# One decoder step on one core: x's spill and four early loads tied to the order of the program, the dt product and the first scores later

## The chip, the cores and the metric

The kernel runs on one core of one Trainium2 chip. The metric is the device time of one execution in microseconds (us). Each kernel is run several times and the median counts.

## The reference

One step of a hybrid decoder layer, in float32, for 256 prompt rows and 8 × 4 = 32 sample rows at once (T = 288 rows, model width 2048). `h` is the normed input. `w_in` projects it to z, x|B|C, dt, q, k, v. Two parallel halves follow: a state-space half (causal convolution, then a scan with a state per head) and a sliding-window attention half. Their joined output goes through `w_out`; then come a cross attention over a memory and a SwiGLU feed-forward, each with its residual.

```python
proj = h @ lp['w_in']
z, xbc, dt_raw, q, k, v = jnp.split(proj, [s1, s2, s3, s4, s5], axis=-1)
xbc, conv_new = causal_conv(xbc, conv0, lp['conv_w'], lp['conv_b'])
dt = jax.nn.softplus(dt_raw + lp['dt_bias'])
y, ssm_new = ssd_scan(xs, dt, a, bm, cm, ssm0)          # state per head
y = rmsnorm((y + xs * d_skip) * silu(z), gate_norm)
att = swa_banded(q, k, v, sinks)                        # prompt rows
att = swa_cached(q, kcat, vcat, pos, k_pos, sinks)      # sample rows, with the key cache
out = concat([y, att]) @ lp['w_out']
x = x + out
x = x + cross_attn(rmsnorm(x), mk, mv, lp)
x = x + ffn(rmsnorm(x), lp)
```

## The kernel before, in words

**Layout and matmuls.** Activations lie with the 2048 model columns on partitions: 16 tiles of 128 × 288. Every weight product is made of three passes (`mm3`, lines 164 to 168): the weight and the activation are each split into a high and a low part in a shorter float format, and lo·hi, hi·hi and hi·lo are summed. A weight **chunk** is 128 × 1024 numbers (512 KB). `wload` (line 139) loads it into a `raw` buffer (3 of them), ACT casts it to `hi` (line 156), DVE subtracts to get `lo` (the helper on line 79); there are 4 buffers of each. A chunk feeds 24 matmuls.

**Order.** The program is written as a sequence, and a scheduler reorders it: it has a time model, gives each engine and queue a fixed order by priority (place in the program, less an offset), and puts in an instruction as soon as the model says that its inputs are there. On the chip each engine then works through its own list in that order and waits where an input is late. Weight loads have an offset of 4000 (they go as soon as a `raw` buffer is free), the splits one of 70. Loads without such an offset, but with nothing to wait for, go as early as a buffer of their pool is free.

**Postponed work.** `later(n, fn)` (line 122) queues `fn` for n steps ahead, and each weight chunk that has been used is one step (`gemm_w`, line 179, which runs half of what is due at a chunk's end and the rest after the next chunk's first half). So the small work of attention and states stands between the matmuls of later chunks.

**The stages around the change.**
- Lines 336 to 360: x is loaded in four column parts, transposed by PE (`split_x`, line 277), split into hi and lo (`xh`, `xl`), and kept in float32 in 16 buffers `xb` (`xst`). Line 291 writes each of these to DRAM (`xspill`) by a DMA that POOL issues; line 1005 reads them back for the residual, long after. In the same loop the chunks of k, v and of the first queries are used.
- Lines 410 to 487: dt. `wdt` (16 columns) is loaded by SP (line 415) and scaled on DVE, 16 small matmuls with `xst` follow (line 421), then `dt_natural`, `dt_softplus` and `dt_sums` are postponed. `dt_sums` writes `csrow` to DRAM; `decay` (line 752) reads it back.
- Lines 494 to 563: queries in four pairs (`rp`). The first pair's product is made with k and v; the other three take 4 chunks each. `swa_prompt` turns each query tile (lines 496 to 500, DVE and POOL) and postpones `scores` (line 503: 8 matmuls on line 511, softmax on DVE and ACT), then `values` and `combine`, which writes `att`. `att` takes over the 16 `xb` buffers of `xst`.
- Line 566: `swa_sample`, the sample rows' attention. It loads the key cache (line 571), transposes it, and stores it to the output by POOL (line 575).
- Line 662: `conv_state` loads the convolution state (line 666) and transposes it.
- Lines 847 to 916: `sample_state(g)` goes through the state of the 8 sample sequences in four tiles of 4 × 256 KB (g, hb): `load` (line 850, loads on line 854), `grow` (POOL: state × decay, written to `m` from `ld` by the helper on line 79), `trans` (PE transposes, DVE adds, SP stores on line 893), `read`.
- `ssd` (line 780) makes, per head pair, `decayed` inputs on POOL (`s` from `s`, 128 × 256), which the PE products on lines 814 and 820 wait for.

The buffers `ld` (6) serve x, `wdt`, the convolution state, the key cache, the states and later the memory. All loads named here are issued by SP, which also issues all weight loads and most stores.

Of the kernel before, what the change touches and what calls it, by code (L numbers as in the profile page):

```python
# [8 lines left out]
F32 = mybir.dt.float32  # L9
# [6 lines left out]
P = 128  # L16
# [30 lines left out]
def tile_hymba_step(ctx: ExitStack, tc: tile.TileContext, I: dict, O: list, stop: int = 99):  # L47
# [24 lines left out]
    def psum(tag="ps"):  # L72
        return tl(p_ps, [P, 512], F32, "ps")
# [41 lines left out]
    def transpose(out, in_):  # L115
        k = in_.shape[0]
        b = in_.base_partition() if callable(in_.base_partition) else in_.base_partition
        nc.tensor.transpose(out, in_, ident[b:b + k, 0:k])  # L118

    pend, clock = [], [0]  # L120
# [156 lines left out]
    def split_x(cp, pcs):  # L277
        pss = []
        for k in range(4):
            kk = cp * 4 + k  # L280
            ps = psum()
            pss.append(ps)
            for t3 in range(3):
                n = P if t3 < 2 else TS
                transpose(ps[:, t3 * P:t3 * P + n], pcs[t3][:n, k * P:(k + 1) * P])
            act(xh[kk], ps[:, :T], AF.Copy, scale=nwcol(V_MIX, kk))
            stt(xl[kk], ps[:, :T], nwcol(V_MIX, kk), f32(xh[kk]), ALU.mult, ALU.subtract)
        for k in range(4):
            st = tl(p_xb, [P, T], F32, "xb")
            nc.vector.tensor_copy(st, pss[k][:, :T])  # L290
            nc.gpsimd.dma_start(xspill[cp * 4 + k], st)
            xst.append(st)
# [35 lines left out]

    # keys, values and the first queries
    wq = w_in.rearrange("(k p) c -> p k c", p=P)  # L330
# [78 lines left out]

    # dt path  # L410
    nat = ts(192).rearrange("p (c j h) -> p c j h", c=3, j=4)
    csrow = tc.dram_tile([16, T], F32, name="csrow")
    wdt = tl(p_ld, [P, 512], F32, "ld").rearrange("p (k h) -> p k h", h=32)
    nc.gpsimd.memset(wdt, 0.0)
    nc.sync.dma_start(wdt[:, :, 0:16], wq[:, :, O_DT:O_DT + 16])
    tt(nc.vector, wdt, wdt, vT[:, 0:KC].unsqueeze(2).to_broadcast([P, KC, 32]), ALU.mult)
    nc.gpsimd.memset(nat, 0.0)
    pdt = psum()
    for k in range(KC):
        j = k % 4  # L420
        nc.tensor.matmul(pdt[32 * j:32 * j + 32, :T], wdt[:, k], xst[k], start=(k < 4), stop=(k >= KC - 4))
    dtT = ts()
    nc.scalar.copy(dtT, pdt[:, :T])
    dx, dy, dz, dp = ts(192).rearrange("p (i c h) -> i p c h", i=4, c=3)
# [60 lines left out]

    later(1, dt_natural)
    later(7, dt_sums)

    # prompt sliding-window attention
    att = [(tl(p_xb, [P, T], F32R, "xb"), tl(p_xb, [P, T], F32R, "xb")) for _ in range(8)]  # L490
# [3 lines left out]
    def swa_prompt(r, pq):  # L494
# [59 lines left out]

        later(1, scores)

# [7 lines left out]

    # sample sliding-window attention
    def swa_sample():
        ms = cst[:, C_MS:C_MS + 144]
        kcT, vc = [], []
        for hb in range(2):
            k_ = tl(p_ld, [P, 4, P], F32, "ld")  # L570
            nc.sync.dma_start(k_, ck[4 * hb:4 * hb + 4].rearrange("b t g d -> t b (g d)"))
            ps = psum()
            for b in range(4):
                transpose(ps[:, b * P:(b + 1) * P], k_[:, b])
            nc.gpsimd.dma_start(o_sk[0, 4 * hb:4 * hb + 4, 0:124].rearrange("b t g d -> t b (g d)"), k_[4:128])
            kt_ = tm()
            nc.scalar.copy(kt_, ps)
            v_ = tm()
            nc.sync.dma_start(v_.rearrange("p (b c) -> p b c", b=4),
                                cv[4 * hb:4 * hb + 4].rearrange("b t g d -> t b (g d)"))  # L580
            nc.gpsimd.dma_start(o_sv[0, 4 * hb:4 * hb + 4, 0:124].rearrange("b t g d -> t b (g d)"),
                                v_[4:128].rearrange("p (b c) -> p b c", b=4))
            kcT += [kt_[:, b * P:(b + 1) * P] for b in range(4)]
            vc += [v_[:, b * P:(b + 1) * P] for b in range(4)]
# [64 lines left out]
        later(3, stage2)  # L649

    later(7, swa_sample)
    if stop <= 1:
# [4 lines left out]

    # state-space heads
    xc = [ts() for _ in range(12)]
    scT = ts().rearrange("p (c k) -> p c k", k=24)  # L660

    def conv_state():
        ps = psum()
        for cp in range(3):
            scv = tl(p_ld, [P, 512], F32, "ld")
            nc.sync.dma_start(scv[:24], I["state_conv"][0, :, :, 512 * cp:512 * cp + 512].rearrange("b k c -> (b k) c"))
            for c in range(4):
                transpose(ps[:, (4 * cp + c) * 24:(4 * cp + c) * 24 + 24], scv[:24, c * P:(c + 1) * P])
        nc.scalar.copy(scT.rearrange("p a b -> p (a b)"), ps[:, :288])
# [172 lines left out]

    # sample states
    bm = cst[:TS, C_BM:C_BM + 8]
    ssm = I["state_ssm"][0].rearrange("b (i f) p n -> i (f p) b n", f=2)
    osm = o_sssm[0].rearrange("b (i f) p n -> i (f p) b n", f=2)
    def sample_state(g):
        py = psum()

        def load(hb):  # L850
            h0s = []
            for i4 in range(4):
                h0 = tl(p_ld, [P, 4, P], F32, "ld")
                nc.sync.dma_start(h0, ssm[4 * g + i4, :, 4 * hb:4 * hb + 4])
                h0s.append(h0)
# [72 lines left out]

    # gate and group norm
    ymx = []  # L930
# [149 lines left out]

    # cross attention
    oT = [(tl(p_xb, [P, T], F32R, "xb"), tl(p_xb, [P, T], F32R, "xb")) for h in range(4)]
# [186 lines left out]

    # feed-forward  # L1270
    NF = DFF // P
# [45 lines left out]

    # final norm
    ydst = [o_yp[0, 0:P], o_yp[0, P:TP], o_ys.rearrange("b t d -> (b t) d")]
# [110 lines left out]
```

## Time and profile before

| | |
|---|---|
| median of 3 runs | 1395.02 us (1394.44 to 1398.37) |
| profiled execution, span from first to last instruction | 1393.4 us; no other time of its own is given |
| PE / DVE / ACT / POOL busy | 99% / 58% / 46% / 13% of the span |
| DMA | 241.17 MB, mean 173 GB/s |

How to read it: PE's busy share counts a matmul as busy from its start to a modelled end, so 99% is not a rate. The rate is read from the start times of the matmuls, and what stands still from the idle times in brackets. The granted clock is a share of TensorE's 2.4 GHz; 0.50 is 1.2 GHz.

### The profile page before, as it was taken

What the parts mean: (1) busy time and instruction counts of PE and PEld (TensorE: products, weight loads), DVE (VectorE), ACT (ScalarE), POOL (GpSimd) and SP (SyncE); (2) the same over time, 40 slices, a digit from 0 to 9 for tenths busy, and PEclk for the clock granted to TensorE, in tenths of its full rate; (3) what the DMA queues carried; (4) which work ended last, traced back from release to release, by engine and by line L of the source; (5) the groups of instructions that cost most, each with busy time, mean ns of one, the idle gap of its engine ahead of it and who ended that gap; (6) DMA issues with size and microseconds to landing.
All of it is one profiled execution on the core that took longest, in us unless ns stands there. A gap on an engine that the chain in (4) does not pass through costs nothing.

```text
span 1393.4 us, 26184 instructions
## 1 busy us (share of the span) xinstructions
PE 1373.9 (99%) x10637; PEld 1338.3 (96%) x10637; DVE 809.1 (58%) x1341; ACT 635.1 (46%) x998; POOL 177.2 (13%) x273
## 2 busy tenths in 40 slices
PE   9899999999999999999999999999999999999997
PEld 8799988899998899999999999999999999999997
DVE  6777798766666559544544544444454554545554
ACT  6355776554555556433433433333343333434332
POOL 4311476403220113000000000000000000000110
PEclk9999999999999999999999999999999999999999
DMA  9655547667657745555555545555555555555552
GB/s 291 169 157 144 150 120 231 187 195 206 185 192 243 228 155 161 166 166 167 162 170 166 166 160 164 165 165 174 167 167 167 167 167 167 167 159 167 166 167 91
DMA packets 249856, 241.17 MB, mean 173 GB/s; under 512 B 12778, under 2 KB 240528, under 8 KB 249736
## 3 DMA queue, kind: packets, MB, share of 16 engines
q1 hardware_dynamic: 246120, 232.43, 54.9%
q0 software_dynamic: 3584, 7.06, 1.7%
q8 instruction: 83, 1.36, 0.4%
q14 instruction: 37, 0.30, 0.1%
q10 hardware_dynamic: 32, 0.01, 0.0%
HBM read 227.59 MB, written 11.85 MB: 172 GB/s over the span
## 4 chain that ended last, share of the span: by engine, by line
PE 87%; DVE 5%; DMA 2%; ACT 2%; issue 2%; POOL 0%; SPq 0%; DVEq 0%; ACTq 0%; POOLq 0%
PE mm L166 27%; PE mm L167 27%; PE mm L168 27%; PE ps L118 2%; DMA raw<-in_w_in_dram 2%; DVE lo L79 2%; DVE s L82 1%; ACT hi L156 1%; PE ps L511 1%; DVE xa L82 1%; DVE m L769 0%; PE ps L1134 0%; DVE s L79 0%; ACT L85 0%; ACT s L85 0%
## 5 line engine op out<-in xcount | busy, mean ns | idle before, releaser
L79 DVE TENSOR_TENSOR lo<-raw,hi 128x1024 fp32r<-128x1024 f32 (+1 forms) x413 | 483.0, 1172 | 472.7 <-ACT hi L156 466.3
L156 ACT CAST hi<-raw 128x1024 fp32r<-128x1024 f32 (+1 forms) x413 | 410.9, 998 | 547.4 <-PE mm L168 435.6
L166 PE MATMUL mm<-xa,lo 128*128 128x288 f32 x2016 | 601.2, 298 | 0.0
L167 PE MATMUL mm<-xa,hi 128*128 128x288 f32 x2016 | 597.5, 296 | 0.0
L168 PE MATMUL mm<-xa,hi 128*128 128x288 f32 x2016 | 591.0, 293 | 0.0
L166 PEld LDWEIGHTS mm<-xa,lo 128*128 128x128 f32 x2016 | 378.4, 188 | 4.7 <-issue 3.8
L168 PEld LDWEIGHTS mm<-xa,hi 128*128 128x128 f32 x2016 | 379.7, 188 | 0.7 <-issue 0.6
L167 PEld LDWEIGHTS mm<-xa,hi 128*128 128x128 f32 x2016 | 379.4, 188 | 1.0 <-issue 0.7
L79 POOL TENSOR_TENSOR ssum<-ssum,ls 128x288 f32<-128x288 f32 x43 | 46.9, 1091 | 880.0 <-ACT ls L85 879.1
L166 PE MATMUL mm<-ls,lo 128*128 128x288 f32 x512 | 152.0, 297 | 0.0
L168 PE MATMUL mm<-ls,hi 128*128 128x288 f32 x512 | 151.4, 296 | 0.0
L167 PE MATMUL mm<-ls,hi 128*128 128x288 f32 x512 | 151.1, 295 | 0.0
L167 PE MATMUL mm<-xb,hi 128*128 128x288 f32 x448 | 132.5, 296 | 0.0
L166 PE MATMUL mm<-xb,lo 128*128 128x288 f32 x448 | 132.1, 295 | 0.0
L168 PE MATMUL mm<-xb,hi 128*128 128x288 f32 x448 | 132.1, 295 | 0.0
L166 PEld LDWEIGHTS mm<-ls,lo 128*128 128x128 f32 x512 | 96.2, 188 | 0.1
L168 PEld LDWEIGHTS mm<-ls,hi 128*128 128x128 f32 x512 | 96.2, 188 | 0.0
L167 PEld LDWEIGHTS mm<-ls,hi 128*128 128x128 f32 x512 | 96.1, 188 | 0.1
L168 PEld LDWEIGHTS mm<-xb,hi 128*128 128x128 f32 x448 | 84.6, 189 | 0.2 <-DVE xb L79 0.2
L166 PEld LDWEIGHTS mm<-xb,lo 128*128 128x128 f32 x448 | 84.5, 189 | 0.1
L167 PEld LDWEIGHTS mm<-xb,hi 128*128 128x128 f32 x448 | 84.0, 188 | 0.1
L79 DVE TENSOR_TENSOR xT<-xT,mm 128x288 f32<-128x288 f32 x64 | 28.2, 448 | 39.1 <-PE mm L168 36.2
(304 smaller groups left out, 1211.3 us busy)
## 6 DMA issues: line engine op xcount, KB each, us to landing
raw<-in_w_gate_dram SPq DMA_DIRECT2D x88, 512.0 KB, 3.6
raw<-in_w_up_dram SPq DMA_DIRECT2D x88, 512.0 KB, 3.6
raw<-in_w_down_dram SPq DMA_DIRECT2D x80, 512.0 KB, 3.5
raw<-in_w_in_dram SPq DMA_DIRECT2D x43, 512.0 KB, 3.9
raw<-in_w_in_dram SPq DMA_DIRECT2D x34, 256.0 KB, 5.3
raw<-in_w_out_dram SPq DMA_DIRECT2D x32, 256.0 KB, 4.1
raw<-in_w_out_dram SPq DMA_DIRECT2D x16, 512.0 KB, 3.6
ld<-in_state_ssm_dram SPq DMA_DIRECT2D x16, 256.0 KB, 4.1
```

Source lines behind the costliest of these rows:

```text
L79: eng.tensor_tensor(out=out, in0=in0, in1=in1, op=op)
L82: nc.vector.scalar_tensor_tensor(out=out, in0=in0, scalar=s, in1=in1, op0=op0, op1=op1)
L118: nc.tensor.transpose(out, in_, ident[b:b + k, 0:k])
L156: nc.scalar.copy(h_, src)
L166: nc.tensor.matmul(ps, wl, xh, start=start, stop=False)
L167: nc.tensor.matmul(ps, wh, xh, start=False, stop=False)
L168: nc.tensor.matmul(ps, wh, xl, start=False, stop=stop)
L511: nc.tensor.matmul(pss[g][:, oc], qa[gs, qc], kT[gs, kc], start=True, stop=True)
```

## The change

A helper `in_turn` calls the scheduler's `keep_in_program_order`: the instruction may stand on its engine's list only behind the instruction of that engine that the program named just before it. It adds an order, not a wait. With it:
- x's spill leaves `split_x` and POOL. It is postponed from the dt product, two tiles per step over 8 steps, issued by SP, each in turn.
- The dt product (16 matmuls and a copy) is postponed by 2 chunks, and `dt_natural` and `dt_sums` count from there.
- The first scores of each query tile come 2 chunks after it, not 1.
- The loads of `wdt`, of the key cache, of the convolution state and of the first state tile (g = 0, hb = 0) are in turn. The key cache's load gets a function of its own, 4 steps ahead of `swa_sample`.

```diff
+    def in_turn(ins):
+        tc.keep_in_program_order(ins)
...
             nc.vector.tensor_copy(st, pss[k][:, :T])
-            nc.gpsimd.dma_start(xspill[cp * 4 + k], st)
...
-    nc.sync.dma_start(wdt[:, :, 0:16], wq[:, :, O_DT:O_DT + 16])
+    in_turn(nc.sync.dma_start(wdt[:, :, 0:16], wq[:, :, O_DT:O_DT + 16]))
...
-    pdt = psum()
-    for k in range(KC):
-        j = k % 4
-        nc.tensor.matmul(pdt[32 * j:32 * j + 32, :T], wdt[:, k], xst[k], start=(k < 4), stop=(k >= KC - 4))
     dtT = ts()
-    nc.scalar.copy(dtT, pdt[:, :T])
+    def dt_product():
+        pdt = psum()
+        for k in range(KC):
+            j = k % 4
+            nc.tensor.matmul(pdt[32 * j:32 * j + 32, :T], wdt[:, k], xst[k], start=(k < 4), stop=(k >= KC - 4))
+        nc.scalar.copy(dtT, pdt[:, :T])
+        for k in range(KC):
+            later(1 + k // 2, lambda k=k: in_turn(nc.sync.dma_start(xspill[k], xst[k])))
+        later(1, dt_natural)
+        later(7, dt_sums)
...
-    later(1, dt_natural)
-    later(7, dt_sums)
+    later(2, dt_product)
...
-        later(1, scores)
+        later(2, scores)
...
+    def cache_keys():
+        for hb in range(2):
+            k_ = tl(p_ld, [P, 4, P], F32, "ld")
+            in_turn(nc.sync.dma_start(k_, ck[4 * hb:4 * hb + 4].rearrange("b t g d -> t b (g d)")))
+            kcs.append(k_)
...
+    later(3, cache_keys)
     later(7, swa_sample)
...
-            nc.sync.dma_start(scv[:24], I["state_conv"][0, :, :, 512 * cp:512 * cp + 512].rearrange("b k c -> (b k) c"))
+            in_turn(nc.sync.dma_start(scv[:24], I["state_conv"][0, :, :, 512 * cp:512 * cp + 512].rearrange(
+                "b k c -> (b k) c")))
...
-                nc.sync.dma_start(h0, ssm[4 * g + i4, :, 4 * hb:4 * hb + 4])
+                ld = nc.sync.dma_start(h0, ssm[4 * g + i4, :, 4 * hb:4 * hb + 4])
+                if g == 0 and hb == 0:
+                    in_turn(ld)
```

## Rows read from the trace of the kernel before

**Rows 1.** Busy time by stretch: us; PE, PEld, DVE, ACT, POOL; clock; DMA share; GB/s.
```profile
0.00:60.00 60.00, 55.47 (x394) 50.08 (x394) 40.61 (x105) 31.62 (x70) 20.04 (x38) 1.00 0.95 263
60.00:65.00 5.00, 4.33 (x22) 3.10 (x23) 4.59 (x22) 2.37 (x12) 3.76 (x8) 0.68 0.16 47
60.00:100.00 40.00, 39.33 (x309) 35.17 (x310) 32.45 (x124) 20.63 (x68) 9.58 (x17) 0.96 0.48 142
180.00:200.00 20.00, 16.86 (x120) 14.97 (x119) 19.95 (x34) 12.59 (x25) 17.02 (x18) 0.87 0.44 130
195.00:200.00 5.00, 3.85 (x12) 2.84 (x13) 4.95 (x4) 0.92 (x4) 5.00 (x5) 0.50 0.48 128
200.00:205.00 5.00, 5.00 (x36) 4.52 (x35) 4.94 (x18) 3.98 (x8) 1.84 (x3) 0.82 0.26 87
```

**Rows 2.** Timeline of PE: start, us, line, operation, count; in brackets idle before, releaser.
```profile
49.61 0.30 PE L167 MATMUL mm<-xa,hi 128*128 128x288 f32 x1
49.75 0.29 PE L168 MATMUL mm<-xa,hi 128*128 128x288 f32 x1
...
60.67 0.93 PE L511 MATMUL ps<-s,s 64*128 64x128 f32 x8 [4.06 <-DVE s L79]
...
107.80 0.92 PE L118 MATMUL ps<-cst,ld 24*128 24x24 f32 x12
...
195.06 1.22 PE L814 MATMUL ps<-s,s 128*128 128x256 f32 x2 [2.04 <-POOL s L79]
...
219.93 0.60 PE L118 MATMUL ps<-cst,ld 128*128 128x128 f32 x4
```

**Rows 3.** Chain of waits, 40 to 60 us: start, us, what.
```profile
50.62 7.98 DMA raw<-in_w_in_dram
...
59.34 0.69 DVE lo L79
```

**Rows 4.** The page's DMA issues: operation, count, KB each, us to landing.
```profile
xspill<-xb POOLq DMA_DIRECT2D x16, 144.0 KB, 5.1
out_dram<-ld POOLq DMA_DIRECT2D x2, 248.0 KB, 10.2
```

**Rows 5.** Timeline of SP's queue: start, us, line, operation, count.
```profile
30.88 0.45 SPq L415 DMA_DIRECT2D ld<-in_w_in_dram  x1
...
46.70 0.37 SPq L854 DMA_DIRECT2D ld<-in_state_ssm_dram  x1
...
89.85 0.82 SPq L754 DMA_DIRECT2D csb<-csrow  x2
92.66 14.18 SPq L147 DMA_DIRECT2D raw<-in_w_in_dram  x4
108.25 1.47 SPq L854 DMA_DIRECT2D ld<-in_state_ssm_dram  x3
...
209.11 0.47 SPq L705 DMA_DIRECT2D out_dram<-s  x1
```

**Rows 6.** Timeline of POOL: start, us, line, operation, count; idle before, releaser.
```profile
146.08 1.57 POOL L581 DMA_DIRECT2D out_dram<-m  x1 [14.82 <-DMA m<-in_cache_swa_v_dram]
...
188.55 5.65 POOL L79 TENSOR_TENSOR m<-ld,s 128x512 f32<-128x512 f32 x4
194.16 4.96 POOL L79 TENSOR_TENSOR s<-s,s 128x256 f32<-128x256 f32 x4
...
223.76 0.45 POOL L79 TENSOR_TENSOR s<-s,s 32x128 f32<-32x128 f32 x1 [4.30 <-ACT s L85]
```

**Rows 7.** Timeline of DVE: start, us, line, operation, count; idle before, releaser.
```profile
191.94 1.35 DVE L82 SCALAR_TENSOR_TENSOR s<-s,cwT,s 128x312 f32<-128x312 f32 x1
...
208.58 0.53 DVE L82 SCALAR_TENSOR_TENSOR s<-s,cwT,s 128x312 f32<-128x312 f32 x1
...
224.52 1.50 DVE L79 TENSOR_TENSOR m<-m,ps 128x512 f32<-128x512 f32 x2 [1.87 <-PE ps L890]
```

**Rows 8.** State loads, line 854: us from issue to landing, min, median, max.
```profile
DMA to landing us min/median/max: 3.8/4.1/10.1
```

More of the change, by code (lines that the diff above doesn't have):

```diff
@@ L563, in tile_hymba_step @@
             swa_prompt(2 * rp + m, pq[m])
+    kcs = []
+    def cache_keys():
[3 more added lines that the diff above has]
+            kcs.append(k_)
     def swa_sample():
@@ L569, in swa_sample @@
         for hb in range(2):
-            k_ = tl(p_ld, [P, 4, P], F32, "ld")
-            nc.sync.dma_start(k_, ck[4 * hb:4 * hb + 4].rearrange("b t g d -> t b (g d)"))
+            k_ = kcs[hb]
             ps = psum()
```

## The prediction

> **What bounds the kernel now.** I first read the windows, for the stretches in which something is slow [rows 1]. The reader is to see three things. In the first 60 us the DMA engines are 95% busy; from 60 to 100 us they are 48% busy. In two stretches, 60 to 65 and 195 to 205 us, the granted clock falls to 0.50 for a time. And from 180 to 200 us DVE is busy 19.95 of 20 us. Then the timeline of PE [rows 2]. Two neighbouring matmuls of a weight chunk start 0.13 to 0.14 us apart, so a chunk of 24 takes some 3.15 us, and wherever they follow like this PE itself is the bound: that is most of the span. What can be won is where they don't. PE stands still for 4.06 us before the first scores at 60.67 us, and for 2.04 us before the state product at 195.06 us, with a further 1.09 us among the products behind it (PE is busy 3.85 of 5.00 us from 195 to 200, and 0.06 of the rest belongs to the first wait).
>
> **The first hole.** Its releaser is a DVE step, the turned query tile that the scores read. Following the chain [rows 3], that step stands on DVE's list behind the `lo` of a weight chunk (59.34 us), and that chunk's transfer took 7.98 us from 50.62 us on. PE has matmuls of loaded chunks left, but its list has the scores first. The transfer is slow because others are under way: by then the spill has put 16 × 144 KB into the busy stretch, the key cache's store 2 × 248 KB with 10.2 us to landing [rows 4], and one state tile went out at 46.70 us [rows 5]. After the hole the clock is 0.68 over 5 us [rows 1], which costs 0.32 × 5 = 1.6 us. **Hole one: 4.06 + 1.6 = 5.7 us.**
>
> **The second hole.** PE waits for POOL's four `decayed` steps, which start at 194.16 us because POOL's list has the four `grow` steps of the first state tile ahead of them, 5.65 us from 188.55 us on [rows 6]. Those aren't due then: the tile's transposes stand at 219.93 us [rows 2]. They got there because the tile was loaded long ago, at 46.70 and 108.25 us [rows 5]. The clock then costs 0.50 × 3.85 + 0.18 × 5 = 2.8 us [rows 1]. **Hole two: 2.04 + 1.09 + 2.8 = 5.9 us.**
>
> **The change part by part.**
>
> *Spill.* Sixteen POOL issues and 2.36 MB leave the stage in which x is loaded. At the stretch's 263 GB/s for a 0.95 share [rows 1], 277 GB/s in full, they are 8.5 us of transfer. They come back as 16 SP issues, which at 0.4 us each (a 0.37 and a 0.45 us issue in [rows 5]) are 6.4 us on a queue that mostly waits for buffers, two per chunk. Each stands behind the weight loads that the program names before it, which run ahead of PE by the three `raw` and four split buffers. The weight loads behind a spill wait 0.4 us each to be issued; ACT's and DVE's splits wait for those, and PE only if its lead of several chunks is used up. From 60 to 100 us the DMA engines have half their time free. Cost between 0 (that lead) and 8.5 us (no lead at all); I take 0, as the 48% row is nearest. `att` takes over the x buffers, so its first writes wait for a spill: `combine` of the first tiles comes at step 6, their spills at 3 and 4, three chunks or some 9 us apart against 5.1 us to landing [rows 4]. Hidden.
>
> *dt product two chunks later.* The same 16 matmuls; PE does weight chunks in their place. Its followers slip by 2 × 3.15 = 6.3 us. The read back of `csrow` is issued at 89.85 us [rows 5], and the first `decay` that uses it is due at step 21, 12 chunks or some 38 us behind `dt_sums` at its new step 9. Hidden; without that cover it would be 6.3 us at most. SP's read would stand in front of weight loads and wait for `csrow`, as it does now.
>
> *Scores one chunk later.* Nobody waits for them but `values` and `combine`, whose result is needed only by the output projection. PE gains 3.15 us of matmuls to do before it may wait. Zero by itself; it helps to close hole one if the chunk is still late.
>
> *`wdt`.* Its load already stands behind the weights of the first queries, at 30.88 us [rows 5]. No move, 0; its DVE scaling waits as before.
>
> *Convolution state and key cache.* Three loads of 48 KB go behind the last query chunk's weights, two of 256 KB behind the third chunk of the stage after it, whose weights go between 92.66 and 107 us [rows 5]. The state's transposes stand at 107.80 us [rows 2], the keys' four chunks behind their load. The last query chunk is issued before 92.66 us, so both have 12 us or more to land: hidden; the price without that cover is a landing, some 5 us as for the spill [rows 4]. The key cache's store moves with them to about 140 us; POOL is idle for 14.82 us before 146.08 us [rows 6], against two issues of about 1.57 us. Hidden.
>
> *First state tile.* Its four loads go behind a store of the convolution's output that the program names before them, at 209.11 us [rows 5]; that store waits for its own data, and the loads with it. So they issue until about 209.6 + 4 × 0.37 = 211.1 us and land some 4.1 us later [rows 8], at 215.2. `grow` can't be at 188.55 us any more and hole two goes, 5.9 us. `grow` now comes from 215 us on. Behind the next `decayed` steps POOL has 4.30 us idle [rows 6]; 5.65 − 4.30 = 1.35 us are not covered. DVE's addition behind it then waits, and PE for its PSUM. It also slows DVE: one convolution step takes 1.35 us beside `grow` and 0.53 us elsewhere [rows 7]. Four such steps, one to a `grow`, are 4 × 0.82 = 3.3 us, of which 1.87 us fall in DVE's idle time before 224.52 us [rows 7]: 1.4 us. Later cost 1.35 + 1.4 = 2.75 us; its ends are 0 and 5.65 + 3.3 = 9.0 us. I take 2.75, since the two idle rows are from the very place.
>
> The Trainium skill, "SBUF — State Buffer", section "SBUF: two separate sides", says that DVE with two SBUF inputs and a reading GpSimd operation exclude each other for a whole instruction. Whole `grow` steps of 5.65 / 4 = 1.41 us on DVE would make 4 × 1.41 − 1.87 = 3.8 us of the 1.4, and the forecast 1388.6 us; the rows show 0.82 us, a little over half, so I stay with them.
>
> **The sum.** 5.7 + 5.9 − 2.75 = 8.85 us. On the profiled execution's span, 1393.4 − 8.9 = 1384.5 us. The median of the runs is 1.6 us above that span, and no closer time of that execution is given; so 1395.0 − 8.8 = **1386.2 us**.
>
> **The rivals.** About 0.3% (4.2 us) is what a measurement of this kernel can tell from no change; below 1390.8 us is faster, above 1399.2 slower.
>
> *Only the first hole closes* (1395.0 − 5.7 = 1389.3 us). For: the second tile's loads are not tied, so its `grow` could take the place that the first one leaves; and DVE is full from 180 to 200 us [rows 1], so a PE that no longer waits for POOL would soon wait for `lo`. Against: with no `grow` beside it DVE is faster there too.
>
> *The spill meets the weights* (1395.0 − 8.85 + 8.5 = 1394.7 us). The bytes are not saved, only moved onto the queue that carries the weights, and the tied loads go out hardly later, because the weight loads they are tied to run far ahead: the change then does in part not what it says. For: the first spills follow the weights of the third query chunk, which are issued inside the busy stretch. Against: the half-empty 60 to 100 us. The Trainium skill, "DMA: Bandwidth & Descriptors", section "Queues, rings and completion order", says that a DMA engine takes turns between queue rows, but works through one row's ring in order; by that, a spill on SP's row holds back the weights behind it, where POOL's row shared. It points to this rival.
>
> *The state tiles come just in time, and late* (slower). The place is PE's list from 219.93 us on: four tile steps, each `load`, `grow`, transposes, store, in buffers that the step before must free. Now the first one has been loaded 100 us ahead. If it lands late, all four slip, PE waits at the transposes, and each step shows its landing of 4.1 us [rows 8]: 16.4 us against the two holes' 11.6, and with half clock after each wait, some 3 us at 0.50 as now, 4 × 1.5 more: 1395.0 − 11.6 + 16.4 + 6.0 = 1405.8 us. It decides from a landing of 219.9 − 211.1 = 8.8 us on; the longest now is 10.1, the median 4.1.
>
> **How the numbers follow.** Forecast 0.44, only the first hole 0.20: both are faster, 0.64. The spill case is within 0.3%: 0.22. The late tiles are slower: 0.14. The first is the likeliest, because both holes have a named cause that the change takes away. The range begins at 1383.0 us, which is both holes without later cost (1395.0 − 11.6 = 1383.4) less the 0.6 us by which the fastest run lies under the median, rounded. It reaches past the spill case at 1394.7 to 1397.0, half of the way into the later cost's upper end; the late tiles stay out.
>
> **What would show it.** Right: no idle time of PE before the first line 511; the clock at 1.00 from 60 to 65 us; the raw transfers around 50 us landing in 4 to 6 us; SP issuing all spills between 40 and 90 us; line 854's first four loads after 200 us; POOL's `decayed` steps with no `m<-ld,s` ahead of them, and PE without idle time at line 814. Wrong: PE waits at line 118 with `ld` as its input after 200 us, or `lo` waiting for raw transfers between 50 and 90 us, or a `grow` still ahead of the first `decayed` steps.

## The result and the profile after

The changed kernel takes 1400.65 us (median of 6 runs, 1398.87 to 1402.85), the kernel before 1395.19 us beside it (6 runs); the ratio is 1.0041, 95% interval 1.0025 to 1.0056. The forecast was 1386.2 us, faster: it is slower, by 5.5 us. The profiled execution of the changed kernel took 1402.85 us, with a span of 1401.1 us.

Every run lists its span and mean granted clock, and (1 − clock) × span is an estimate of the time that half clock cost it; it is an upper one, since PE also waits in part of that time, and the clock is listed to three places. Over the 6 runs it is 11.9 us of a mean span of 1399.0; over the 114 runs of the kernel before that the experiments share, 8.0 of 1392.9. So of 6.0 us of span, up to 3.9 are clock, and some 2.1 are left for waits. The two profiles say the same of the waits: PE stands still for 14.3 us of the first 600 in the changed kernel and for 12.1 in the kernel before.

Line numbers grow by up to 19: 511 is now 519, 814 and 820 are 831 and 837, 854 is 871. The windows of the changed kernel, as in [rows 1]:

```profile
60.00:65.00 5.00, 5.00 (x38) 4.61 (x38) 4.96 (x29) 4.27 (x20) 1.59 (x4) 1.00 0.67 228
60.00:100.00 40.00, 40.00 (x330) 37.02 (x330) 36.68 (x141) 23.74 (x81) 10.08 (x14) 1.00 0.61 179
160.00:180.00 20.00, 20.00 (x139) 18.59 (x138) 14.07 (x46) 12.55 (x21) 7.57 (x14) 0.83 0.45 136
195.00:200.00 5.00, 3.73 (x28) 3.52 (x29) 3.31 (x9) 2.94 (x7) 2.27 (x3) 1.00 0.73 204
210.00:230.00 20.00, 16.18 (x99) 14.72 (x99) 12.45 (x26) 12.26 (x24) 11.41 (x17) 0.83 0.62 179
240.00:260.00 20.00, 15.95 (x114) 14.21 (x113) 14.06 (x20) 7.11 (x14) 12.70 (x17) 0.83 0.42 115
```

Three of these stretches in the kernel before:

```profile
160.00:180.00 20.00, 19.93 (x162) 18.13 (x161) 18.46 (x48) 15.67 (x28) 12.30 (x19) 1.00 0.43 124
210.00:230.00 20.00, 18.76 (x168) 17.28 (x167) 16.48 (x30) 13.57 (x24) 12.12 (x17) 1.00 0.82 237
240.00:260.00 20.00, 18.58 (x170) 17.09 (x170) 17.56 (x26) 9.42 (x20) 13.94 (x20) 1.00 0.56 162
```

The clock is full from 60 to 65 us and around 195 us, where the kernel before had 0.68 and 0.50. But in this execution it falls in three stretches where it had not, by 0.17 × 20 = 3.4 us each. The timeline of PE in the changed kernel, its longer waits from 50 to 250 us:

```profile
56.89 0.89 PE L519 MATMUL ps<-s,s 64*128 64x128 f32 x4 [0.81 <-DVE s L79]
...
193.66 0.70 PE L831 MATMUL ps<-s,s 128*128 128x256 f32 x2 [0.88 <-POOL s L79]
195.21 0.49 PE L837 MATMUL ps<-s,s 128*128 128x128 f32 x2 [0.85 <-POOL s L79]
196.76 0.94 PE L837 MATMUL ps<-s,s 128*128 128x128 f32 x6 [1.06 <-POOL s L79]
...
216.88 0.70 PE L831 MATMUL ps<-s,s 128*128 128x256 f32 x2 [2.63 <-POOL s L79]
219.19 1.22 PE L837 MATMUL ps<-s,s 128*128 128x128 f32 x4 [1.20 <-POOL s L79]
...
247.89 0.70 PE L831 MATMUL ps<-s,s 128*128 128x256 f32 x2 [2.98 <-POOL s L79]
```

The first hole [rows 2] is down from 4.06 to 0.81 us. The second still has 0.88 + 0.85 + 1.06 us, and there are two new ones, before the state products of the second and third head pair. All wait for POOL. POOL's list in the changed kernel, against [rows 6]:

```profile
191.50 1.29 POOL L79 TENSOR_TENSOR m<-m,s 128x512 f32<-128x512 f32 x1 [1.83 <-ACT m L85]
192.75 4.52 POOL L79 TENSOR_TENSOR s<-s,s 128x256 f32<-128x256 f32 x4
...
206.30 4.31 POOL L79 TENSOR_TENSOR m<-ld,s 128x512 f32<-128x512 f32 x3 [3.00 <-DMA ld<-in_state_ssm_dram]
215.13 1.07 POOL L79 TENSOR_TENSOR m<-ld,s 128x512 f32<-128x512 f32 x1 [4.03 <-DMA ld<-in_state_ssm_dram]
216.16 3.54 POOL L79 TENSOR_TENSOR s<-s,s 128x256 f32<-128x256 f32 x4
...
240.00 6.04 POOL L79 TENSOR_TENSOR m<-ld,s 128x512 f32<-128x512 f32 x4
...
247.00 3.98 POOL L79 TENSOR_TENSOR s<-s,s 128x256 f32<-128x256 f32 x4
```

`grow` (`m<-ld,s`) again stands ahead of `decayed` (`s<-s,s`, 128x256), twice: at 206.30 us that of the tied tile, whose last step waits 4.03 us for its load, and at 240.00 us that of a later tile. Why the tied tile's last load is late stands in SP's queue [rows 5]:

```profile
203.25 1.50 SPq L871 DMA_DIRECT2D ld<-in_state_ssm_dram  x3
206.03 2.81 SPq L150 DMA_DIRECT2D raw<-in_w_in_dram  x2
208.90 1.60 SPq L871 DMA_DIRECT2D ld<-in_state_ssm_dram  x3
```

The fourth load stands behind two weight loads and goes out only at 208.90 us, 5.7 us after the first. The one landing that is listed for line 871 took 6.1 us, against a median of 4.1 [rows 8].

### The profile page after: what moved, and what is told of

It is laid out like the page before. It is cut to its first block, busy times and chain, and to the rows that moved or that the text cites. A ratio compares the mean times of both kernels' runs of the same rounds, so it can differ in the third digit from the quotient of the medians.

```text
span 1401.1 us, 26143 instructions
## 1 busy us (share of the span) xinstructions
PE 1379.1 (98%) x10637; PEld 1343.4 (96%) x10637; DVE 806.1 (58%) x1341; ACT 635.6 (45%) x998; POOL 164.6 (12%) x257
## 3 DMA queue, kind: packets, MB, share of 16 engines
q8 instruction: 83, 1.36, 0.4%
## 4 chain that ended last, share of the span: by engine, by line
PE 91%; DVE 3%; DMA 2%; POOL 2%; issue 1%; ACT 1%; SPq 0%; DVEq 0%; ACTq 0%; POOLq 0%
PE mm L169 28%; PE mm L170 27%; PE mm L171 27%; PE ps L118 3%; DVE lo L79 1%; POOL s L79 1%; DMA raw<-in_w_in_dram 1%; ACT hi L159 1%; POOL m L79 1%; DVE xa L82 1%; PE ps L519 1%; DMA ld<-in_state_ssm_dram 0%; PE ps L1153 0%; DMA raw<-in_w_out_dram 0%; PE ps L837 0%
```

## The experiments

In this table "tied" means that the four loads of the first state tile are kept in program order, "free" that they are not. "`grow` folded" means that POOL makes no `grow`: DVE makes state × decay + product in one step per sequence. "Value products" are the products of the softmax weights with the cached values in the sample rows' attention. Times are medians; a ratio is to the kernel before, run beside each, which came to 1394.6 to 1395.3 us each time. "Clock" is the mean of (1 − clock) × span over a kernel's runs.

| kernel | us | ratio, 95% interval | clock, us |
|---|---|---|---|
| e1: change, tile free | 1398.61 | 1.0021 (1.0007 to 1.0034) | 11.3 |
| e2: before, tile tied | 1406.68 | 1.0086 (1.0067 to 1.0105) | 15.9 |
| e3: change, `decayed` first | 1398.44 | 1.0025 (1.0012 to 1.0037) | 10.8 |
| e4: e3, tile free | 1402.46 | 1.0053 (1.0034 to 1.0073) | 14.2 |
| e5: before, `grow` folded | 1389.65 | 0.9965 (0.9952 to 0.9979) | 4.6 |
| e6: change, `grow` folded | 1386.85 | 0.9938 (0.9923 to 0.9952) | 4.6 |
| e7: e1, value stores later | 1394.28 | 0.9989 (0.9978 to 1.0000) | 7.8 |
| e8: e1, no load tied | 1404.73 | 1.0065 (1.0051 to 1.0078) | 15.7 |
| e9: e6, value products spread | 1384.97 | 0.9931 (0.9911 to 0.9952) | 2.8 |
| e10: before, other loads tied | 1391.19 | 0.9976 (0.9963 to 0.9989) | 6.1 |
| e11: change, spill on POOL | 1400.63 | 1.0044 (1.0029 to 1.0059) | 11.7 |
| e12: e10, `grow` folded | 1388.38 | 0.9953 (0.9938 to 0.9969) | 5.1 |
| e13: before, scores later | 1402.25 | 1.0044 (1.0027 to 1.0062) | 14.1 |
| e14: before, dt product later | 1395.61 | 1.0003 (0.9990 to 1.0016) | 8.1 |
| e15: e12, value products spread | 1384.69 | 0.9919 (0.9904 to 0.9934) | 2.5 |
| e16: e15, tile tied | 1389.64 | 0.9962 (0.9947 to 0.9976) | 5.4 |
| e17: change, scores back | 1404.32 | 1.0061 (1.0044 to 1.0078) | 13.3 |
| e18: e17, tile free | 1393.42 | 0.9988 (0.9978 to 0.9999) | 7.2 |

### The tied tile, undone and alone (e1, e2)

e1 takes the two lines out of the changed kernel, e2 puts them into the kernel before:

```diff
+                if g == 0 and hb == 0:
+                    in_turn(ld)
```

> The changed kernel with the first state tile's four loads no longer tied to program order; all else of the change stays. POOL's list then has `grow` of that tile ahead of the first `decayed` steps again, and the later `decayed` steps ahead of or between the halves of `grow`, as in the kernel before. Theory 1 (the tied tile is what costs): the hole before the first scores stays closed, the one at 188 to 195 us comes back, and the waits at the second and third state products (2.63 + 1.20 and 2.98 + 0.85 us, and the half clock behind them) go: 1395.2 - 5.7 = 1389.5 us. Theory 2 (the loss lies in the later schedule of the other parts, the spill on SP above all, and the tile is only where it shows): 1400 us, within 2 us of the changed kernel.

> The kernel before with only the first state tile's four loads tied to program order. Theory 1: the hole before the first scores stays (5.7 us not won), and POOL's waits at 216 and 247 us come as in the changed kernel: 1400.7 + 5.7 = 1406.4 us. Theory 2: the tile's place is worth little by itself: 1395.2 us, within 2 us.

e2 came out at theory 1's figure: the tie alone costs 11.9 us in the kernel before. But e1 stayed at 1398.6, 9 us above its own. So there was a second cause, one that is there without the tie. In e1 the first new wait of PE is in the sample scores, with half clock behind it; the timeline of PE, and the window around:

```profile
148.03 0.65 PE L610 MATMUL ps<-m,s 64*32 64x128 f32 x8 [1.42 <-DVE stx L614]
...
202.41 1.22 PE L831 MATMUL ps<-s,s 128*128 128x256 f32 x2 [2.95 <-POOL s L79]
```
```profile
140.00:160.00 20.00, 18.58 (x127) 16.47 (x126) 11.82 (x36) 14.78 (x28) 6.65 (x18) 0.74 0.57 156
```

DVE, which frees the PSUM of the scores, was late by a convolution step that waited for ACT, and ACT for POOL. On POOL's list both stores of the value cache stand ahead of the convolution's small steps; in the kernel before one of the two stands behind the first of them. The changed kernel has both ahead too, 1.9 us earlier (137.51 us), and its PE doesn't wait there; so the order alone doesn't make the wait. Rows of POOL, of ACT and of DVE in e1:

```profile
139.38 3.06 POOL L596 DMA_DIRECT2D out_dram<-m  x2 [14.79 <-issue]
142.43 0.12 POOL L697 MEMSET s<- 128x3 f32 x1
```
```profile
142.72 0.65 ACT L85 ACTIVATE s<-s,vT,cwT 128x312 f32<-128x312 f32 x1 [3.34 <-POOL s L706]
```
```profile
143.41 1.12 DVE L82 SCALAR_TENSOR_TENSOR s<-s,cwT,s 128x312 f32<-128x312 f32 x2 [4.87 <-ACT s L85]
```

### POOL's order by hand (e3, e4)

```diff
-            tt(nc.gpsimd, hv_(o_), hv_(src), ...
+            in_turn(nc.gpsimd.tensor_tensor(out=hv_(o_), in0=hv_(src), op=ALU.mult, in1=...
...
-                tt(nc.gpsimd, hn.rearrange("p (b n) -> p b n", b=4), h0s[i4], ...
+                in_turn(nc.gpsimd.tensor_tensor(out=hn.rearrange("p (b n) -> p b n", b=4), in0=h0s[i4], ...
```

> The changed kernel with POOL's `grow` and `decayed` steps also kept in program order, so that every `grow` stands behind the `decayed` steps that the program names before it. Theory 1 in its narrower form (the late load costs only because `grow` waits for it ahead of `decayed` on POOL's list): PE's idle time before the second and third state products goes, 2.63 + 1.20 and 2.98 + 0.85 + 0.23 us, and the half clock behind each, 0.34 x 10 us twice, 14.7 us in all: 1400.7 - 14.7 = 1386.0 us, and no `decayed` behind a `grow` that waits for a DMA. Rival (the tile itself is late, whatever stands behind it): the waits move to the tile's transposes or to DVE's addition: 1400 us, within 3 us.

> As the run before, and the first tile's loads not tied. The tile is then there early, and `grow` stands behind `decayed` all the same. Theory 1 in its narrower form: the same 1386.0 us, or up to 2.8 us less if the landing still showed anywhere. Rival (late tile): this one alone is fast, 1386 us, where the run before stays at 1400. Theory 2 (the other parts): both stay at 1395 to 1400 us.

Neither came to 1386. The waits for `decayed` at the second and third state products went, as expected, but another took their place, at the tile's transposes, whether the tile was early (e4, 4.35 us) or late (e3). e4 has the wait in the sample scores besides (1.51 us at 148.74 us). So at the transposes it is not the landing but something behind it. POOL, DVE and PE in e3:

```profile
213.18 4.06 POOL L890 TENSOR_TENSOR m<-ld,s 128x512 f32<-128x512 f32 x4
```
```profile
212.67 4.92 DVE L82 SCALAR_TENSOR_TENSOR s<-s,cwT,s 128x312 f32<-128x312 f32 x1
```
```profile
222.91 1.09 PE L118 MATMUL ps<-cst,ld 128*128 128x128 f32 x4 [4.34 <-DVE m L79]
```

One convolution step of DVE, 0.53 us elsewhere [rows 7], took 4.92 us: as long as four `grow` steps in a row. From there DVE has no idle time up to its addition at 222.18 us, which is late by that and releases the PSUM that the transposes need. e4 has the same step, 4.92 us from 215.24 us on.

### The other parts, one by one (e7, e8, e10, e11, e13, e14, e17, e18)

e7 postpones the value cache's stores; e8 drops `in_turn` from `wdt`, key cache and convolution state as well; e10 adds just these three ties, with `cache_keys`, to the kernel before; e11 puts the spill's line back into `split_x`. e13 and e14 each make one postponement of the change in the kernel before, e17 takes the scores' back, e18 the scores' and the tile's:

```diff
-            nc.gpsimd.dma_start(o_sv[0, 4 * hb:4 * hb + 4, 0:124]...
+            later(2, lambda hb=hb, v_=v_: in_turn(nc.gpsimd.dma_start(o_sv[0, 4 * hb:4 * hb + 4, 0:124]...
...
-        later(1, scores)
+        later(2, scores)
...
+    later(2, dt_product)
```

> The first run's kernel (changed kernel, tile free), with the two stores of the value cache issued by POOL two chunks later, so that the convolution's small POOL steps don't stand behind the wait for the value cache and its 2 x 1.53 us of issue. Theory: PE's 1.42 us wait in the sample scores at 148 us, and the 5.1 us that the half clock costs behind it, come from there and go: 1398.6 - 6.5 = 1392.1 us. Rival (the wait comes from DVE's or ACT's own work): 1398.6 us, within 1.5 us, with the wait at the same place.

> The changed kernel without any tied load but the spill's: the later dt product, the later spill on SP and the later scores stay, the loads of the dt weights, the key cache, the convolution state and the first tile float as before. Theory (spill, dt product and scores close the first hole by themselves): PE waits 0.9 us or less before the first scores, and the second hole is as in the first run. If the tied key cache and convolution state make the value cache late and with it the 1.42 us wait and its half clock, these go: 1392 us. If not, the time is that of the first run: 1398.6 us. Rival (the first hole closes only because loads no longer go out early): 4 us idle before the first scores again.

> The kernel before with only the dt weights', the key cache's and the convolution state's loads tied; the spill stays on POOL, dt product and scores stay where they were, the first tile floats. Theory (the ties close the first hole, not the spill or the scores): PE's 4.06 us before the first scores and the half clock behind go, most of 5.7 us; and if the later value cache then stands in front of the convolution's POOL steps, the 1.42 us wait and 5.1 us of half clock of the first run come: 1396.0 us; without that, 1389.5 us. Rival (later scores or the spill close the hole): 4 us idle stays, 1395 us or more.

> The changed kernel with the spill undone alone: its sixteen stores are issued by POOL as x is loaded, as in the kernel before. If the spill's new place costs nothing, as forecast, the time is the changed kernel's or, should the first hole open again, up to 5.7 us more: 1400.7 to 1406.4 us. If the stores on SP hold up the weights: down to 1392.2 us (8.5 us less).

> The kernel before with only the scores one chunk later. Theory A (this step alone turns POOL's list over: both value-cache stores ahead of the convolution's steps, and `grow`, two convolution steps and a decay ahead of the first `decayed`): the waits of the run without ties, 1.4 to 1.6 us in the sample scores and some 3 us at the first state product, with their half clock, and some 3 us before the first scores: 1404.7 us, within 2 us. Theory B (the later dt product does it): 1395.2 us, or up to 5.7 us less if the later scores close the first hole.

> The kernel before with only the dt product two chunks later; the spill stays on POOL in its old place. Theory A (the scores are the step that costs): 1395.2 us, within 1.5 us, with POOL's list as before. Theory B (the dt product is): 1404.7 us, within 2 us.

> The changed kernel with the first scores one chunk later undone alone; the tied tile and all else stay. Theory (either edit turns POOL's list over; with the tile tied, the list is the changed kernel's whether the scores are later or not): 1400.7 us, within 2 us. Rival (the two act by separate waits that add): 1393 to 1396 us.

> The changed kernel with both the later scores and the tied tile undone; the ties of dt weights, key cache and convolution state, the spill on SP and the later dt product stay. Theory: POOL's list is that of the kernel before, the first hole is closed by the ties, and the time is that of the ties alone: 1391.2 us, within 1.5 us. Rival (the spill on SP or the later dt product costs where the list is right): 1395 us or more.

e7: the wait at 148 us and the half clock behind it are gone, 4.3 us of the 6.5 expected. e10: three ties, of `wdt`, key cache and convolution state, close the first hole alone, and the kernel is faster, 1391.2 us. `wdt` keeps its place in SP's queue (30.55 us, against 30.88 before), so it is the other two, which no run separates. Without them (e8) 3.05 us of the hole stay, though spill and scores are moved, and the time is 1404.7 us, 6.1 above the higher of the two figures expected, that of e1. How large the hole was to begin with varies: e5, whose SP queue up to 60 us has the order of the kernel before, shows 2.60 and 0.24 us there, at full clock from 60 to 65 us, in place of 4.06 us and 0.68. PE in e10 and in e5:

```profile
58.22 1.15 PE L514 MATMUL ps<-s,s 64*128 64x128 f32 x8 [0.23 <-DVE s L79]
```
```profile
59.01 0.93 PE L511 MATMUL ps<-s,s 64*128 64x128 f32 x8 [2.60 <-DVE s L79]
```

e11: in the changed kernel the spill's place is worth nothing. e14: nor is the dt product's in the kernel before. e13: the scores one chunk later cost 7.6 us by themselves, 2.4 less than theory A had. PE in e13:

```profile
58.51 0.93 PE L511 MATMUL ps<-s,s 64*128 64x128 f32 x8 [2.59 <-DVE s L79]
151.00 0.42 PE L595 MATMUL ps<-m,s 64*32 64x128 f32 x8 [1.36 <-DVE stx L599]
...
204.23 1.22 PE L814 MATMUL ps<-s,s 128*128 128x256 f32 x2 [2.96 <-POOL s L79]
```

That is e1's pattern. POOL's list in e13 has the same turned order as e1 and e8: both value stores ahead of the convolution steps, and the four `grow` steps, one tile's convolution steps and a decay ahead of the first `decayed`. In e10, e14 and e18 it is that of the kernel before. In e2 and e17, where the tile is tied and the scores are not later, both value stores stand ahead as well, and PE waits 1.19 and 1.36 us in the sample scores: either edit turns this part of the list. What `grow` costs there shows on DVE in e1 (POOL's rows first):

```profile
187.47 1.28 POOL L79 TENSOR_TENSOR m<-m,s 128x512 f32<-128x512 f32 x1
188.72 4.06 POOL L79 TENSOR_TENSOR m<-ld,s 128x512 f32<-128x512 f32 x4
...
201.50 4.52 POOL L79 TENSOR_TENSOR s<-s,s 128x256 f32<-128x256 f32 x4
```
```profile
187.47 5.67 DVE L82 SCALAR_TENSOR_TENSOR s<-s,cwT,s 128x312 f32<-128x312 f32 x1
```

One DVE step stood for 5.67 us, all of five POOL steps. POOL, done with `grow` at 192.78, then waits 2.81 us for DVE and 1.82 us for a decay's exponential from ACT, and starts `decayed` only at 201.50 us. The changed kernel has the same two waits (2.81 and 1.83 us) without `grow` in front of them, and starts it at 192.75. That DVE's late step is what keeps the exponentials late in e1 is argued from this order, not tested.

e17 and e18 close the account. With the other ties, the spill and the dt product in place, four kernels differ by two edits: neither 1393.4 (e18), later scores alone 1398.6 (e1), tied tile alone 1404.3 (e17), both 1400.7 (the changed kernel). Each is enough to make it slow, they don't add, and undoing one leaves it slow. The table shows this; that both act through POOL's list is argued from the lists. e17 is 3.6 us above the figure expected, but far from the rival's. e18 is 2.2 us above e10; whether spill and dt product cost that much together is not settled, the ratios' intervals overlap.

### `grow` off POOL (e5, e6, e12), the value products spread (e9, e15), and the tile's tie with both (e16)

```diff
-                tt(nc.gpsimd, hn.rearrange("p (b n) -> p b n", b=4), h0s[i4],
-                   ecs[4 * g + i4][:, e_:e_ + 13:4].unsqueeze(2).to_broadcast([P, 4, P]), ALU.mult)
...
-                tt(nc.vector, hn, hn, ps, ALU.add)
+                for b in range(4):
+                    stt(hn[:, b * P:(b + 1) * P], h0[:, b], es[b], ps[:, b * P:(b + 1) * P], ALU.mult, ALU.add)
...
-            for hb in range(2):
+            for hb in hbs:
...
+            if hbs[-1] == 0:
+                return later(1, lambda: combine(pts2, po, [1]))
```

> The kernel before with `grow` taken off POOL: DVE makes state x decay + product in one step per sequence (four 128 x 128 steps instead of one 128 x 512 addition), nothing else is changed and no load is tied. If `grow` in front of `decayed` on POOL's list makes the second hole, and POOL's `grow` beside DVE the slow DVE steps after it, 2.04 + 1.09 us idle and 2.8 us of half clock go, and the waits of 1.02 and 0.91 us behind the first tile: 1395.2 - 7.8 = 1387.4 us. Rival: what `decayed` waits for is the exponential of the decay before it, which DVE's full stretch from 180 to 200 us makes late; then an idle time of some 2.8 us stays at the state products, with its clock, and the time is 1393 us or more.

> The changed kernel with the same edit: no `grow` on POOL, all of the change stays, the tied tile too. Theory (the tied tile costs through POOL's list alone): the idle time at the second and third state products (2.63 + 1.20 and 2.98 + 0.85 + 0.23 us) and the half clock behind each (3.4 us twice) go: 1400.7 - 14.7 = 1386.0 us. Rival (the tile itself is late, so the wait moves to its transposes or to DVE's step): 1396 us or more, with PE waiting at the transposes with `ld` as input. Second rival (the clock falls anyway, in the sample attention at 165 us and behind whatever wait is left): 1390 to 1394 us.

> The kernel before with the ties of dt weights, key cache and convolution state, and `grow` folded into DVE's step; spill, dt product, scores and first tile as before. If the two gains add (first hole by the ties, 4.06 + 1.6 us; second by the folded step, 5.6 us as measured): 1395.2 - 5.7 - 5.6 = 1383.9 us. Rival (the sample attention pays for the tied key cache with a wait at 148 us and its half clock, 6.5 us): 1390.4 us.

> The changed kernel with `grow` folded into DVE's step, and the value products of the sample attention in two steps, one half of the sequences a chunk of weights later than the other. Theory: the half clock that starts inside these products at 165 us in the changed kernel, in the folded one and in several others (some 3.4 us in each) follows four groups of products of 32 columns that stand too close together; apart, it goes: 1386.9 - 3.4 = 1383.5 us. Rival (it follows from something else in that stretch, or comes back at another place): 1386.9 us, within 1.5 us, with 0.78 and 0.88 or like values at 160 to 180 us.

> The kernel before with the ties of dt weights, key cache and convolution state, `grow` folded into DVE's step and the sample attention's value products in two steps; the first tile floats, spill, dt product and scores as before. Its like without the split products took 1388.4 us and its like with all of the change 1385.0 us. If the split takes 1.9 us as it did there: 1386.5 us. If the early tile still costs (PE's 2.5 us wait on ACT at the first state products), it stays 1.5 us above the next run.

> As the run before, with the first tile tied too; spill, dt product and scores stay as in the kernel before. If with `grow` off POOL neither the moved spill nor the moved scores matter, this is the folded and split form of the changed kernel: 1385.0 us, within 1.5 us. If the later scores still cost by the order of the convolution's steps, it is faster than that: 1382 us. If the ties alone, without later scores, leave the first hole open: 1388 us or more.

e6 came to 1386.85 us where 1386.0 was worked out from the waits and the clock behind them: in the changed kernel the waits at the second and third state products, and the half clock behind them, go through `grow` on POOL. Two windows of e6:

```profile
210.00:230.00 20.00, 19.01 (x180) 16.91 (x179) 14.45 (x37) 11.79 (x23) 5.83 (x15) 1.00 0.86 246
240.00:260.00 20.00, 20.00 (x164) 18.43 (x163) 15.64 (x38) 12.27 (x25) 6.28 (x11) 1.00 0.59 175
```

e5 gains 5.6 us in the kernel before, between its two figures: a wait of 2.51 us for ACT takes the hole's place. e12, with the three ties added, is 1.3 us faster than e5, so the two gains don't add (1383.9 us was expected of that): the wait for ACT is still there. PE in e5; e12 has it at 195.21 us with 2.50:

```profile
197.54 0.72 PE L833 MATMUL ps<-s,s 128*64 128x128 f32 x8 [2.51 <-ACT s L816]
```

What stays in e6 is the half clock from 160 to 180 us. In the changed kernel it begins inside the value products of the sample attention, and PE isn't idle in the 8 us before it; e6 and e3 show the same (PE, two of these groups, 1.06 for 0.65 us at half clock, and the window behind them):

```profile
165.85 0.65 PE L649 MATMUL ps<-m,m 128*64 128x32 f32 x8
...
167.50 1.06 PE L649 MATMUL ps<-m,m 128*64 128x32 f32 x8
```
```profile
168.00:174.00 6.00, 6.00 (x29) 5.94 (x29) 4.19 (x9) 3.51 (x6) 3.94 (x5) 0.50 0.59 176
```

Spread over two chunks (e9) the same stretch has full clock, but the next one, with two waits of PE for POOL (0.87 and 1.06 us), has 0.91, where e6 has 1.00:

```profile
160.00:180.00 20.00, 20.00 (x173) 18.17 (x172) 17.69 (x47) 15.91 (x27) 11.92 (x18) 1.00 0.47 139
180.00:200.00 20.00, 18.07 (x134) 16.46 (x132) 18.32 (x42) 16.28 (x30) 12.23 (x16) 0.91 0.45 137
```

e9 gains 1.9 us, not 3.4; 0.09 × 20 = 1.8 us came back at the other place. Its runs lie within 1.2 us (1384.46 to 1385.65), where e6's span 5.7 us and the fastest of e6 lists a clock of 0.999, under 1.4 us lost in all: the half clock in the products comes in some executions only. e9's theory is thus not shown: the kernel before has the same products, not spread, at 168.67 us at full clock in its profile, and so has e12:

```profile
160.00:180.00 20.00, 20.00 (x174) 18.18 (x173) 18.81 (x52) 15.80 (x27) 12.10 (x18) 1.00 0.50 145
```

e15, the kernel before with the three other ties, `grow` folded and the products spread, is as fast as e9 and the fastest measured, 1384.69 us. e16 adds the tied tile alone and is 5 us slower, so that much of the tie doesn't go through `grow`. Its profile, of the slowest of its twelve runs, shows two routes: a wait for DVE at the scores, 0.35 us in e15, and the turned order of the value stores with its wait in the sample scores. POOL and PE in e16:

```profile
145.77 3.07 POOL L591 DMA_DIRECT2D out_dram<-m  x2 [13.72 <-DMA m<-in_cache_swa_v_dram]
```
```profile
114.52 1.65 PE L514 MATMUL ps<-s,s 64*128 64x128 f32 x6 [2.84 <-DVE xb L79]
...
154.41 0.49 PE L605 MATMUL ps<-m,s 64*32 64x128 f32 x8 [1.09 <-DVE stx L609]
```

What its other runs, 1387.0 to 1391.2 us, have of these is not on record.

## Why the prediction was wrong

Term by term, in the two profiled executions, whose spans differ by 7.7 us:

| term of the sum | forecast, us | profiles, us |
|---|---|---|
| first hole | −5.7 | −4.9 |
| second hole | −5.9 | −3.1 |
| later cost of the first state tile, here at the second and third state products | +2.75 | +11.2 (4.4 idle, 6.8 clock) |
| half clock in the value products | none | +3.4 |
| a wait for DVE at 318.89 us | none | +1.1 |

**First hole: right in the profiles, but its price was one execution's.** 3.25 of 4.06 us and the clock's 1.6 were won, against 5.7. The tied key cache and convolution state do it alone (e10, 0.23 us left), the tied tile does much of it (e2, 1.22 and 0.24), the later scores don't (e13, 2.59; e5, which changes nothing there, has 2.60). In medians it is worth less: e10 gains 3.9 us, and e18, with all but the two edits that cost, 1.2.

**Second hole: half right.** The clock's 2.8 us were won, of the idle 3.13 us only 0.34. With `grow` gone, `decayed` stood behind a decay step that waited 1.83 us for ACT's exponential. The sum took the whole wait of 3.13 us away and had no term for what would be late next.

**Scores one chunk later, "Zero by itself": the first step that failed.** It costs 7.6 us alone (e13). The prediction priced what waits for the scores, not what a chunk's shift does to the order of the other lists: POOL's turned over 80 us further on.

**First state tile, 2.75 us: the second, and in the changed kernel the larger.** It costs 11.9 us alone (e2), 10.9 in e17 against e18. The step that failed is "Behind the next `decayed` steps POOL has 4.30 us idle": this took `decayed` to come first and `grow` to fill the idle time. The list has `grow` first, its last load is late, and everything behind it waits, PE's products too. Two half clock stretches follow, 3.4 us each, and the sum had none. The time of the landing was right, by luck in its parts: 215.2 us was forecast, and the last `grow` step gets its tile at 215.13, with the load out earlier (208.90, not 211.1) and 6.1 us under way, not 4.1.

**DVE beside `grow`, 0.82 us a step: right at the first tile, not a bound.** In the changed kernel a convolution step beside that tile's `grow` took 1.33 us, 0.80 over its 0.53:

```profile
208.37 1.33 DVE L82 SCALAR_TENSOR_TENSOR s<-s,cwT,s 128x312 f32<-128x312 f32 x1
```

Beside a later tile's `grow` one took 2.21 us (245.16 us). In other kernels, beside POOL steps in a row, one DVE step took 4.4 us (e3, e4) or 5.1 us (e1) more than its 0.53. The Trainium skill, "SBUF — State Buffer", section "SBUF: two separate sides", has the two exclude each other for a whole instruction; the prediction set that aside for the row. The 4.92 and 5.67 us agree with the page and go past it, a whole series of POOL instructions for one DVE step.

**Spill, dt product, `wdt`: right**, the spill with e11 (1400.63 us, against 1400.65), the dt product with e14 (1395.61 us, against 1394.68). `wdt` was not changed alone; its load is at 29.00 us, behind the same weights. The rival of the spill meeting the weights falls.

**The slower rival** had the sign and the edit, but not the place. It looked for PE waiting at the transposes from 219.93 us on, and decided by a landing of 8.8 us. The landing was 6.1, and POOL, which works in order between tile and state products, was already late.

The upper end of the range doesn't come out of its own terms: half of 9.0 − 2.75 beyond 1394.7 is 1397.8 us, not 1397.0. The measured time lies outside either.

## What to carry to other kernels

When a step is moved under a scheduler that fixes each engine's list, compare the lists of all engines before and after, above all what an in-order engine now has ahead of the step that PE waits for; in this kernel the price of two moves was there, not at the step. A load tied to come just in time makes its first reader a wait for all that stands behind it, so take that reader off the shared list first: here folding `grow` into DVE's step turned the same change from 5.5 us slower into 8.4 us faster (e6), of which 5.6 us come without the change (e5). Nothing here gained from tying the tile: e15 leaves it free and is as fast as e9. And count half clock apart from idle time: up to 3.9 of the 6.0 us lost were clock.

## What was not expected of the hardware

- Beside four and five POOL steps in a row, a DVE step of two SBUF inputs took 4.92 (e3, e4) and 5.67 us (e1) in place of 0.53, and each of POOL's `grow` steps 1.02. In [rows 6, 7], where POOL's four `grow` steps also follow without a gap, both were slower by less, 1.35 us for DVE's step and 1.41 for each of POOL's. What decides between the two is not shown.
- TensorE's granted clock fell to 0.50 (1.2 GHz) with PE busy 20.00 of 20 us around it, in a stretch of products of 32 columns. It did not in the profiles with these spread (e9, e15, e16), nor in some with them together (the kernel before, e12); the cause stays open.
- The runs of one kernel differ mostly by clock: over the 114 of the kernel before, the mean granted clock lay between 0.991 and 0.997, which is 0.006 × 1393 = 8.4 us, and the spans between 1387.8 and 1397.4 us, 9.6 us. The clock isn't all of it: the runs that list 0.992 span 5.4 us.
